# Layer 0's output weights split at the start and loaded back in pieces, with the first modulation blocks at high priority

## The chip, the cores and the metric

The kernel runs on one core of one Trainium2 chip. The metric is the device time of one execution in microseconds (us); the median of several runs counts. The engines are TensorE (PE, with its weight loads apart as PEld), VectorE (DVE), ScalarE (ACT), GpSimd (POOL) and SyncE (SP), whose queue issues almost all DMAs.

## What is computed

The reference is a backbone of two layers over 2048 latent tokens and 256 context tokens with 1024 channels (2304 rows in all). Layer 0 feeds a latent attention of 8 heads (MLA) and a bidirectional mLSTM of 4 heads from one projection, layer 1 a gated linear attention and a neighbourhood attention. Each layer modulates its normalised input by a vector from `c`, multiplies the joined heads by a gate and projects them with `w_out`:

```python
cq, ckv, k_rope, mq, mk, mv, mo, gates, z = split_cols(u @ w_in, EVEN_SPLITS)
...
a_lat = block_attention(qa_l, jnp.concatenate([ka_c, ka_l], axis=2), jnp.concatenate([va_c, va_l], axis=2), scale)
...
h_c, h_l = bidirectional_scan(mlstm_chunked, init, seq_c, gates_c, seq_l, gates_l)
...
hm = head_rmsnorm(jax.nn.sigmoid(mo.astype(jnp.float32)) * merge_heads(h), h_norm, MLSTM_HEADS).astype(dtype)
return (jnp.concatenate([merge_heads(a), hm], axis=-1) * jax.nn.silu(z)) @ w_out
```

## The kernel before

Rows are tiled by 128. A float32 matrix product is made of fp16 parts: weights and inputs are scaled by a power of two and split into a high part and the remainder (`wh`, `wl`, `uh`, `ul`), and three products are added in PSUM. For the big input projection (`gemm_in`, "the gemm" below) `weights_` does this for each block of columns: load `wr` (L288), maximum of magnitudes on DVE (L290), scale (`pow2_scale`, L145 to L153: a small chain of PE and DVE), scaling and high part on ACT (L299, L300), remainder on POOL (L301). The products are L322 (columns in the rows, 128x384) and L343 (tokens in the rows, 128x256); their results leave PSUM by ACT (L278) or DVE (L276), and go to DRAM scratch (`scr_mqk`, `scr_rpg` from L328, `scr_z` from L361).

Layer 0's input stage (`layer0_in`) has the following parts. At the opening `prep_u0` computes the modulation (`mods`: `c` is loaded, its tanh taken at L103, 2 MB blocks `wm` of the modulation weights are loaded at L115, multiplied at L122 and gathered at L126 and L133), and its columns (`prep_cols`), and normalises the input (L187, L191, L80 to L87). Then layer 1's output weights are split by `out_weights`: eight loads `owr` of 512 KB (L1001), eight maxima on DVE (L1003), the scale, and for each of the eight the high part on ACT (L1016) and the remainder on DVE (L1017), stored to scratch `w1hl` (L1019). Then come the mLSTM's convolution, gates (L832 to L897, with loads `gbi`, `gA`, `gB` and transposes L887 on PE) and scan (from L951), and the preparation of the latent attention (`mla_prep`: projections L489, keys and queries stored at L498, values by L515, stored at L389).

Then layer 0's own output weights are split by the same function (`out_setup0`), with the results kept in SBUF (`owh`, `owl`) until the projection behind the attention. The attention (`mla_attn`) needs, for each block of 512 queries of a head, the maximum of each query's scores first (`qmax`: matmul L578, DVE maximum L579) and then scores (L613 to L615), exponentials (L618) and values (L633). Keys `kk` are loaded at L561, values `v` at L564, queries `qq` at L569; 34 units of maxima are computed before the main loop. The first `kk` lies in memory that the `owr` buffers of `out_setup0` use before it; the second `kk` lies where layer 0's input `uh`, `ul` was, which the gemm reads to its end. After the lead come the last gemm blocks (`mo` and `z`), and the mLSTM's norm (`mlstm_norm`: loads `hf` L1047, `hb` L1048, `mo` L1049, sum on POOL L1050, product on DVE L1051, norm L1059, store L1060), then the attention's main loop, with PE in an order written by hand. `finish` writes 40 blocks `att0` (5 of each head).

The order of instructions on each queue is set at build time by a scheduler that simulates the engines: it takes code in the order traced, lets later code go ahead where an engine would wait, and lets code under `high_priority` go first. So the gemm is filler: its blocks stand between the parts of the other stages. SBUF pools are placed on two sides; a new tile waits for the last reader of the memory that it takes.

## Time and profile before

| | |
|---|---|
| Median of 3 runs | 3649.45 us (3647.62 to 3654.1) |
| Profiled execution | 3645.0 us, its span 3642.7 us |
| Mean granted clock of PE | 0.974 |
| Busy: PE, DVE, ACT, POOL | 3391.9, 2563.9, 1832.6, 972.9 us |
| Mean DMA rate | 137 GB/s |

In the rows below, "busy" is the time in which an engine works, "idle before <-X" the time that it stood still ahead of an instruction and what ended that. The granted clock is a share of 2.4 GHz. Shares of DMA are those of 16 DMA engines.

### The profile page before, as it was taken

The page shows a single profiled execution, that of the slowest core. Times are in us where ns is not written, and L with a number is a line of the kernel's source. Part 1 is how long each engine was busy: PE and PEld are TensorE (multiplying, and loading weights), DVE is VectorE, ACT ScalarE, POOL GpSimd, SP SyncE. Part 2 cuts the span into 40 slices and gives each one's busy share as a digit, 9 for nine tenths or more (in the row PEclk, how much of TensorE's full clock was granted, in tenths as well). Part 3 has the DMA queues.
Part 4 walks back from the last instruction along what each step waited for, and adds up shares of the span by engine and source line. Part 5 has one row for each costly group of instructions (what it writes and reads, how often), then busy time and mean ns, then how long its engine had stood idle before and what let it go on. Part 6 is the DMA issues. An engine that isn't in the chain of part 4 may idle for free.

```text
span 3642.7 us, 77364 instructions
## 1 busy us (share of the span) xinstructions
PE 3391.9 (93%) x30588; PEld 2575.3 (71%) x30588; DVE 2563.9 (70%) x5697; ACT 1832.6 (50%) x3243; POOL 972.9 (27%) x908
## 2 busy tenths in 40 slices
PE   6999999999888899999999999999888899899898
PEld 3566888898556677777777555676565789898754
DVE  5657576678766888888887566354688547776887
ACT  4333323334443577777777433256465435455632
POOL 1012204473221233333333222101355322111122
PEclk8999999999999799999999999999999999999999
DMA  7632347776778222221110543227554545437343
GB/s 264 242 122 69 141 179 227 222 234 218 215 225 231 77 49 52 53 49 47 31 47 14 168 152 121 66 83 211 166 160 133 144 98 145 123 96 194 117 164 122
DMA packets 400535, 498.35 MB, mean 137 GB/s; under 512 B 104110, under 2 KB 306339, under 8 KB 394988
## 3 DMA queue, kind: packets, MB, share of 16 engines
q1 hardware_dynamic: 400172, 493.40, 44.7%
q8 instruction: 241, 3.95, 0.5%
q14 instruction: 122, 1.00, 0.1%
HBM read 311.73 MB, written 181.43 MB: 135 GB/s over the span
## 4 chain that ended last, share of the span: by engine, by line
PE 58%; DVE 20%; DMA 12%; issue 5%; ACT 4%; POOL 1%; SPq 1%; POOLq 0%; DVEq 0%; ACTq 0%
PE ps L343 13%; PE ps L322 8%; PE po L633 5%; PE ops L1119 4%; PE pm L578 4%; PE ps L613 3%; PE ps L615 3%; PE ps L614 3%; PE t L1544 2%; DVE mc L579 1%; PE s L1522 1%; PE o L1560 1%; PE s L1523 1%; DMA scr_mqkc<-y 1%; PE ps L489 1%
## 5 line engine op out<-in xcount | busy, mean ns | idle before, releaser
L343 PE MATMUL ps<-wh,uh 128*128 128x256 f16 (+3 forms) x2816 | 742.6, 269 | 33.8 <-ACT ot L278 13.0
L343 PE MATMUL ps<-wl,uh 128*128 128x256 f16 (+3 forms) x2816 | 741.6, 268 | 0.0
L343 PE MATMUL ps<-wh,ul 128*128 128x256 f16 (+3 forms) x2816 | 736.3, 268 | 1.4 <-POOL ul L210 1.4
L343 PEld LDWEIGHTS <-uh 128*128 128x128 f16 x5632 | 532.1, 99 | 118.2 <-issue 43.4
L579 DVE TENSOR_REDUCE mc<-pm 128x1 f32<-128x512 f32 (+1 forms) x656 | 403.2, 628 | 115.5 <-PE pm L578 107.3
L618 ACT ACTIVATE p<-ps 128x1024 f32<-128x1024 f32 (+1 forms) x296 | 299.8, 1013 | 158.8 <-PE ps L615 119.2
L322 PE MATMUL ps<-uh,wh 128*128 128x384 f16 (+2 forms) x1008 | 323.9, 325 | 7.5 <-DVE ofs L332 2.8
L322 PE MATMUL ps<-ul,wh 128*128 128x384 f16 (+2 forms) x1008 | 326.1, 326 | 1.1 <-DVE ul L210 1.1
L322 PE MATMUL ps<-uh,wl 128*128 128x384 f16 (+2 forms) x1008 | 325.7, 325 | 0.0
L622 POOL TENSOR_TENSOR pl<-p,ph 128x1024 f16<-128x1024 f32 (+1 forms) x98 | 207.9, 2122 | 434.8 <-ACT ph L619 416.5
L619 ACT CAST ph<-p 128x1024 f16<-128x1024 f32 (+1 forms) x296 | 306.4, 1035 | 7.6
L343 PEld LDWEIGHTS <-ul 128*128 128x128 f16 x2816 | 277.6, 99 | 37.7 <-POOL ul L210 2.6
L322 PEld LDWEIGHTS <-wh 128*128 128x128 f16 (+1 forms) x2016 | 198.2, 100 | 134.8 <-issue 24.0
L578 PE MATMUL pm<-kk,qq 96*128 96x512 f32 (+1 forms) x656 | 271.5, 418 | 21.4 <-DVE mc L579 15.8
L622 DVE TENSOR_TENSOR pl<-p,ph 128x1024 f16<-128x1024 f32 (+1 forms) x198 | 244.4, 1236 | 27.7 <-ACT ph L619 23.0
L301 POOL TENSOR_TENSOR wl<-wr,wh 128x2048 f16<-128x2048 f32 (+4 forms) x31 | 121.3, 3914 | 492.8 <-ACT wh L300 431.0
L633 PE MATMUL po<-v,ph 128*128 128x129 f16 x2336 | 246.8, 221 | 0.0
L613 PE MATMUL ps<-qq,kk 96*128 96x512 f32 (+1 forms) x592 | 240.5, 406 | 0.0
L633 PEld LDWEIGHTS <-pl 128*128 128x128 f16 x2336 | 196.6, 98 | 61.2 <-issue 58.9
L633 PE MATMUL po<-v,pl 128*128 128x65 f16 x2336 | 237.4, 194 | 0.4 <-DVE pl L622 0.4
L615 PE MATMUL ps<-qq,kk 98*128 98x512 f32 (+1 forms) x592 | 233.1, 394 | 0.0
L614 PE MATMUL ps<-qq,kk 96*128 96x512 f32 (+1 forms) x592 | 232.4, 393 | 0.0
(429 smaller groups left out, 7997.3 us busy)
## 6 DMA issues: line engine op xcount, KB each, us to landing
wr<-in_l_w_in_dram SPq DMA_DIRECT2D x26, 1024.0 KB
wm<-in_l_w_mod_dram SPq DMA_DIRECT2D x12, 2048.0 KB
z<-scr_z SPq DMA_DIRECT2D x34, 512.0 KB
scr_z<-ot SPq DMA_DIRECT2D x44, 384.0 KB
k<-scr_nk SPq DMA_DIRECT2D x14, 1152.0 KB
scr_mqk<-of SPq DMA_DIRECT2D x48, 192.0 KB
x<-scr_mqk SPq DMA_DIRECT2D x8, 1152.0 KB
scr_mqkc<-y SPq DMA_DIRECT2D x8, 1152.0 KB
```

What stands on the lines that cost most here:

```text
L322: nc.tensor.matmul(ps[0:m, t0:BLK], w_[:, k, m0:m0 + m], u_[:, k, t0:BLK], start=(q == 0), stop=(q == 3 * KT - 1))
L343: nc.tensor.matmul(ps[:, 0:n], u_[:, k, i * P:(i + 1) * P], w_[:, k, 0:n], start=(q == 0), stop=(q == 3 * KT - 1))
L578: nc.tensor.matmul(pm[:, 0:n], qq[0:96, 0, s * P:(s + 1) * P], kk[0:96, 0, u * 512:u * 512 + n], start=True, stop=True)
L579: nc.vector.reduce_max(mc[:, s, u:u + 1], pm[:, 0:n], AX.X)
L613: nc.tensor.matmul(pj[:, 0:nq], kk[0:96, 0, ks], qq[0:96, 1, 0:nq], start=True, stop=False)
L614: nc.tensor.matmul(pj[:, 0:nq], kk[0:96, 1, ks], qq[0:96, 0, 0:nq], start=False, stop=False)
L615: nc.tensor.matmul(pj[:, 0:nq], kk[0:98, 0, ks], qq[0:98, 0, 0:nq], start=False, stop=True)
L618: nc.scalar.activation(p32[:, :, 0:nq], ps[:, :, 0:nq], AF.Exp, scale=scale)
L619: nc.scalar.copy(ph[:, :, 0:nq], p32[:, :, 0:nq])
L622: eng.tensor_tensor(pl[:, :, 0:nq], p32[:, :, 0:nq], ph[:, :, 0:nq], ALU.subtract)
L633: nc.tensor.matmul(o_, p_[:, j, s * P:(s + 1) * P], v[:, kt, 0:w], start=w == 129 and kt == 0 and s % 2 == 0, stop=w == 129 and kt == kts[ ...
L1119: nc.tensor.matmul(ps, c_[:, k], w_[k][:, ns], start=(q == 0), stop=(q == 3 * KT - 1))
```

## The change

Three things are changed. First, layer 0's output weights are split right after layer 1's, by the same function and into a new DRAM scratch `w0hl`; the scale is kept in a small tile `ows0`. `out_setup0` only takes the SBUF tile `owhl` for them, which has the size of `owh` and `owl`, and it is filled in the attention: 16 loads of 256 KB, one behind each store of `att0` from the sixth on, ordered behind it on SP's queue. Second, in `prep_u0` the two calls of `mods` and `prep_cols` are traced at high priority. Third, the remainder of the input weights on POOL is made in eight pieces for the weights that are traced before `prep_u0` has put its input there (`u[1]` is None), which are the first two; the others keep one instruction.

```diff
             sink = mk(name="pu_mp", bufs=1, space=PSUM).tile([P, 256, 2], F32, name="pmod")[:, 0:16]
-            mods((2, 3), sink)
+            with tc.high_priority():
+                mods((2, 3), sink)
             nxt = load_block(0)
-            mods((0, 1), sink)
-            last = self.dma_mods
-            m4, out[1] = self.prep_cols(0, cp, up, pp, sink)
+            with tc.high_priority():
+                mods((0, 1), sink)
+                last = self.dma_mods
+                m4, out[1] = self.prep_cols(0, cp, up, pp, sink)
...
-            nc.gpsimd.tensor_tensor(wl[:, :, 0:n], wr[:, :, 0:n], wh[:, :, 0:n], ALU.subtract)
+            step = 1 if u[1] is None else KT
+            for k in range(0, KT, step):
+                nc.gpsimd.tensor_tensor(wl[:, k:k + step, 0:n], wr[:, k:k + step, 0:n], wh[:, k:k + step, 0:n], ALU.subtract)
...
+                fin[0] += 1
+                k = fin[0] - 6
+                if 0 <= k < 2 * KT:
+                    with tc.issue_after(st.ins):
+                        nc.sync.dma_start(self.hl0[:, k // KT, k % KT], S["w0hl"][:, k // KT, k % KT])
...
-                self.nc.vector.tensor_copy(self.ows1, self.out_weights(1, xp, xp, ops, S["w1hl"]))
+                for i, ows in ((1, self.ows1), (0, self.ows0)):
+                    self.nc.vector.tensor_copy(ows, self.out_weights(i, xp, xp, ops, S[f"w{i}hl"]))
...
-            w0 = self.out_setup0()
+            *w0, hl = self.out_setup0()
...
-        with tc.tile_pool(name="opx0", bufs=2, side="right") as xp, tc.tile_pool(name="opp0", bufs=2, space=PSUM, side="right") as ops:
-            w = self.out_weights(0, cpw, xp, ops)
-        return e0, cpw, w
+        hl = cpw.tile([P, 2, KT, D], F16, name="owhl")
+        return e0, cpw, ([hl[:, 0, k] for k in range(KT)], [hl[:, 1, k] for k in range(KT)], self.ows0), hl
```

Lines behind the edits move down; L1001 is L1013 in the changed kernel, L1019 is L1024, L561 is L566, L578 is L583, L343 is L348, L613 is L618.

What stands on each engine's queue is shown at three places. The first is ACT's opening, before (`th` is the tanh of `c`, `wr` and `wh` the first weight, `sqj` the normalisation):

```order
L103 ACT_TABLE_LOAD
L103 ACTIVATE th<-c_177 16x128
L299 ACTIVATE wr<-wr,wsc 128x2048
L300 CAST wh<-wr 128x2048
L187 ACTIVATE sqj,ssq<-x 128x1024 x5
```

The same of the changed kernel:

```order
L302 ACT_TABLE_LOAD
L302 ACTIVATE wr<-wr,wsc 128x2048
L104 ACTIVATE th<-c_193 16x128
L303 CAST wh<-wr 128x2048
L188 ACTIVATE sqj,ssq<-x 128x1024 x4
```

The tanh has moved behind the scaling of the first weight; on SP the first `wm` stands ahead of `c`.

The second place is SP's queue at the early split, before (rows 61 on; `scr_mqk` are the gemm's stores, `wr` the gemm's next weight):

```order
L1001 DMA owr<-in_l_w_out_dram 128x1024 x8
L328 DMA scr_mqk<-of 128x384 x6
L1019 DMA scr_w1hl<-ohl 256x1x1024
L328 DMA scr_mqk<-of 128x384
L1019 DMA scr_w1hl<-ohl 256x1x1024
L288 DMA wr<-in_l_w_in_dram 128x8x256
```

Of the changed kernel, from the same load on:

```order
L1013 DMA owr<-in_l_w_out_dram 128x1024 x8
L333 DMA scr_mqk<-of 128x384 x6
L1024 DMA scr_w1hl<-ohl 256x1x1024
L1013 DMA owr<-in_l_w_out_dram 128x1024
L1024 DMA scr_w1hl<-ohl 256x1x1024
L1013 DMA owr<-in_l_w_out_dram 128x1024
L291 DMA wr<-in_l_w_in_dram 128x8x256
```

A load of layer 0's weights now follows each store of layer 1's; eight stores `w0hl` come after these, ahead of the gates' loads. On PE the first transpose of the gates (L887) stands behind 1239 gemm matmuls, where it stood behind 1027.

The third place is SP's queue on the way into the attention, before (`scr_v` are the stores of the values, `gate` and `hm` those of the output stage and the mLSTM):

```order
L1001 DMA owr<-in_l_w_out_dram 128x1024 x6
L389 DMA scr_v_70<-ov_10347 128x8x129
L1001 DMA owr<-in_l_w_out_dram 128x1024 x2
L1048 DMA hb<-scr_h_76 128x512
L139 DMA gate<-scr_mods_57 128x1024
...
L1048 DMA hb<-scr_h_76 128x512
L561 DMA kk_10435<-scr_kn 64x4608
L562 DMA kk_10435<-scr_kr 32x4608
L564 DMA v<-scr_v_70 128x2322 x2
```

Of the changed kernel:

```order
L394 DMA scr_v_70<-ov_10420 128x8x129
L566 DMA kk_10459<-scr_kn 64x4608
L567 DMA kk_10459<-scr_kr 32x4608
L140 DMA gate<-scr_mods_57 128x1024
L1064 DMA scr_hm<-hf 128x512
L394 DMA scr_v_70<-ov_10432 128x8x129
```

The loads of `kk` have moved up to the last store of the values; the eight loads of `owr` are gone from there. On PE, 282 gemm matmuls follow the last L515, where 417 did, and eight of the query maxima stand among them, where two did. In the attention the list differs by the 16 loads alone, and after it in nothing.

## Rows read from the trace of the kernel before

**Rows 1.** page: engines' busy time; shares of the chain that ended last

```profile
PE 3391.9 (93%) x30588; PEld 2575.3 (71%) x30588; DVE 2563.9 (70%) x5697; ACT 1832.6 (50%) x3243; POOL 972.9 (27%) x908
...
PE 58%; DVE 20%; DMA 12%; issue 5%; ACT 4%; POOL 1%; SPq 1%; POOLq 0%; DVEq 0%; ACTq 0%
```

**Rows 2.** windows: PE, PEld, DVE, ACT, POOL busy; clock, DMA share, GB/s

```profile
1128.90:1187.80 58.90, 48.95 (x424) 42.22 (x422) 40.38 (x87) 20.56 (x48) 4.67 (x4) 0.97 0.89 245
1187.80:1219.60 31.80, 21.31 (x38) 9.23 (x37) 25.25 (x61) 3.58 (x15) 3.27 (x2) 0.55 0.49 134
```

**Rows 3.** chain of waits, 1120 to 1225: start us, us, what it is

```profile
1171.25 1.19 DVE owl L1017
...
1173.77 10.49 DMA v<-scr_v
...
1188.98 10.41 DMA hf<-scr_h
...
1220.24 0.43 PE pm L578
```

**Rows 4.** timeline of PE: start, us, engine, line, operation, tiles, count, [idle before]

```profile
1128.78 0.27 PE L343 MATMUL ps<-wh,uh 128*128 128x256 f16 x1
...
1129.98 0.27 PE L343 MATMUL ps<-wh,ul 128*128 128x256 f16 x1
...
1184.32 0.77 PE L578 MATMUL pm<-kk,qq 96*128 96x256 f32 x2 [4.68 <-DMA v<-scr_v]
...
1187.47 0.29 PE L343 MATMUL ps<-wh,ul 128*128 128x256 f16 x1
...
1202.27 0.58 PE L578 MATMUL pm<-kk,qq 96*128 96x256 f32 x1 [3.71 <-DVE mc L579]
1204.58 1.22 PE L578 MATMUL pm<-kk,qq 96*128 96x512 f32 x2 [1.72 <-DVE mc L579]
...
1219.39 0.41 PE L613 MATMUL ps<-qq,kk 96*128 96x256 f32 x1
```

**Rows 5.** timeline of SP's queue, around the loads for the attention

```profile
1131.08 3.92 SPq L1001 DMA_DIRECT2D owr<-in_l_w_out_dram  x6
...
1172.47 0.48 SPq L561 DMA_DIRECT2D kk<-scr_kn  x1
```

**Rows 6.** windows of the mLSTM scan and of the attention's preparation

```profile
560.00:900.00 340.00, 329.21 (x2961) 302.83 (x2959) 235.58 (x779) 137.91 (x403) 171.89 (x231) 0.99 0.72 228
900.00:1130.00 230.00, 199.44 (x1350) 133.47 (x1349) 164.19 (x469) 101.65 (x290) 47.48 (x53) 0.98 0.75 222
```

**Rows 7.** groups of instructions, 160 to 260 us: busy, mean ns | idle before

```profile
L1017 DVE SCALAR_TENSOR_TENSOR ohl<-owr,ows,ohl 128x1024 f16<-128x1024 f32 x8 | 10.2, 1283 | 7.6 <-ACT ohl L1016 7.6
...
L1016 ACT ACTIVATE ohl<-owr,ows 128x1024 f16<-128x1024 f32 x8 | 9.1, 1146 | 13.4 <-DMA scr_w1hl<-ohl 8.2 <-DVE ows L153 5.1
L1003 DVE TENSOR_REDUCE omx<-owr 128x1 f32<-128x1024 f32 x7 | 8.2, 1212 | 0.0
```

**Rows 8.** windows of the gemm around the early split, of the attention

```profile
160.00:240.00 80.00, 80.00 (x493) 50.72 (x491) 36.24 (x70) 32.49 (x32) 13.51 (x5) 1.00 0.50 170
...
1440.00:1980.00 540.00, 529.05 (x4809) 420.81 (x4807) 456.33 (x711) 421.42 (x451) 181.40 (x119) 1.00 0.17 41
```

**Rows 9.** timeline of the opening, by engine: PE, ACT, DVE, POOL

```profile
12.14 3.64 PE L122 MATMUL mps<-wm,sT 128*32 128x512 f32 x16 [1.20 <-DMA wm<-in_l_w_mod_dram]
...
50.55 0.58 PE L151 MATMUL ps<-pw_sc,ones 1*128 1x2 f32 x2 [4.45 <-DVE pw_sc L150]
...
6.34 1.28 ACT L103 ACT_TABLE_LOAD   x1 [6.34 <-DMA c<-in_c_ctx_dram]
...
11.18 2.00 ACT L299 ACTIVATE wr<-wr,wsc 128x2048 f32<-128x2048 f32 x1 [3.23 <-DVE wsc L153]
...
46.35 3.69 DVE L85 TENSOR_TENSOR rs_t<-rstd 128x3 f32<-128x3 f32 x1
...
45.94 4.08 POOL L301 TENSOR_TENSOR wl<-wr,wh 128x2048 f16<-128x2048 f32 x1 [26.69 <-ACT wh L300]
```

More of the change, by code (lines that the diff above doesn't have):

```diff
@@ L73, in __init__ @@
         self.glss = self.const.tile([P, 16, 4], F32, name="glss")
+        self.ows0 = self.const.tile([P, 2], F32, name="ows0")
         self.ows1 = self.const.tile([P, 2], F32, name="ows1")
@@ L600, in qmax_row @@
                     nc.sync.dma_start(qq[96 + a:97 + a, 0, 0:nq].bitcast(F32).rearrange("o (s p) -> o s p", p=P), mt[0:ns, a].bitcast(F32))
-            cnt = [0]
+            cnt, fin = [0], [0]
             def qk(blk, pr, mid):
@@ L650, in finish @@
                 nc.gpsimd.tensor_tensor(ob[:, 0:na], ob[:, 0:na], rc[:, 0:na].broadcast_to([P, na, 2, 64]), ALU.mult)
-                nc.sync.dma_start(S["att0"][q0:q0 + nq, h * 64:(h + 1) * 64].rearrange("(s p) d -> p s d", p=P),
-                                  ob[:, 0:na].rearrange("p a b d -> p (a b) d"))
+                st = nc.sync.dma_start(S["att0"][q0:q0 + nq, h * 64:(h + 1) * 64].rearrange("(s p) d -> p s d", p=P),
+                                       ob[:, 0:na].rearrange("p a b d -> p (a b) d"))
+                fin[0] += 1
[3 more added lines that the diff above has]
+                        nc.sync.dma_start(self.hl0[:, k // KT, k % KT], S["w0hl"][:, k // KT, k % KT])
             todo = []
@@ L783, in layer0_in @@
             self.mlstm_norm()
+        self.hl0 = hl
         return w0, attn
@@ L992, in mlstm_scan, with out_weights @@
                 step(back[i], 1)
-    def out_weights(self, layer, cp, xp, pp, dst=None):
+    def out_weights(self, layer, cp, xp, pp, dst):
         nc, I = self.nc, self.I
@@ L1005, in out_weights @@
         ws = self.pow2_scale(cp, pp, mx[:, KT:KT + 1], "ows", "ops")
-        if dst is None:
-            wh = cp.tile([P, KT, D], F16, name="owh")
-            wl = cp.tile([P, KT, D], F16, name="owl")
         for k in range(KT):
             wr = wrs[k]
-            if dst is None:
-                h, l = wh[:, k], wl[:, k]
-            else:
-                hl = xp.tile([P, 2, D], F16, name="ohl")
-                h, l = hl[:, 0], hl[:, 1]
+            hl = xp.tile([P, 2, D], F16, name="ohl")
+            h, l = hl[:, 0], hl[:, 1]
             nc.scalar.activation(h, wr, AF.Copy, scale=ws[:, 0:1])
             nc.vector.scalar_tensor_tensor(l, wr, ws[:, 0:1], h, ALU.mult, ALU.subtract)
-            if dst is not None:
-                nc.sync.dma_start(dst[:, :, k], hl)
-        return ([wh[:, k] for k in range(KT)], [wl[:, k] for k in range(KT)], ws) if dst is None else ws
+            nc.sync.dma_start(dst[:, :, k], hl)
+        return ws
     def out_setup0(self):
@@ L1710 @@
     "gq": (256, T), "gk": (256, T), "gva": (T, 544), "gla": (SEQ, 512), "glB": (P, 4, T), "glZ": (NT, P, 4, P),
-    "w1hl": ((P, 2, KT, D), F16), "nq": (512, 2, T), "nk": (512, 2, T), "nv16": ((8, P, NT, 129), F16), "z1": (T, 1024), "na": (SEQ, 512),
+    "w0hl": ((P, 2, KT, D), F16), "w1hl": ((P, 2, KT, D), F16), "nq": (512, 2, T), "nk": (512, 2, T), "nv16": ((8, P, NT, 129), F16), "z1": (T, 1024), "na": (SEQ, 512),
 }
```

## The prediction

> **What bounds the kernel now.** I read the page first: busy times and the chain that ended last. TensorE (PE) is busy 93% of the span and holds 58% of the chain, VectorE (DVE) 20% [rows 1]. So an edit can win only where PE stands still, or runs slowly because it stood still; DVE, ACT or DMA time beside a busy PE is worth nothing. Next I looked for the stretches where PE stands still. The one that the change aims at is the passage into layer 0's attention, from the last value projection (L515, its last matmul gives way to gemm at 1128.8 us, T0 below) to the first score matmul L613 at 1219.4 [rows 4]. In its first part PE is busy 48.95 of 58.9 us, in its second 21.31 of 31.8 at a granted clock of 0.55 [rows 2]. What holds it up is told by the chain of waits and SP's queue: `owr` loads go out at 1131.08 and SP hands out the first `kk` load at 1172.47 only, right after the last L1017 has let go of the memory in which `kk` is to lie (1171.25 and 1.19 in the chain) [rows 3, 5]. Then `v` takes 10.49 us and PE waits 4.68 us for it [rows 3, 4]. In the second part, PE waits on the DVE maxima (L579), with one gap around 1202 where DVE itself stood behind an `hf` load of 10.41 us [rows 3, 4].
>
> The sum is made on the profiled execution: 3645.0 us, 2.3 of them outside its span of 3642.7. The median of the runs is 3649.45, so 4.45 us go on top at the end.
>
> **The passage into the attention.** First what it costs now, clean. Between T0 and the first L613 the order has 417 gemm matmuls (L343) and 35 query-maximum matmuls (L578), two of the latter ahead of the last 13 gemm matmuls. A gemm matmul takes 0.109 us (eleven steps between 1128.78 and 1129.98) [rows 4]; a maximum behind the gemm takes 0.82 (18 of them between 1204.58 and 1219.39, paced by DVE) [rows 4]. 417 x 0.109 = 45.5, 33 x 0.82 = 27.1, together 72.6; it took 90.6, so 18.0 us are waits and low clock: 4.7 for `v`, 4.7 in the tail (31.8 - 27.1) [rows 2], 8.6 in the gemm, beside the reductions, the splitting and the `owr` loads.
>
> After the change the `owr` loads, L1003, L1016 and L1017 are gone from there and `kk` stands on SP ahead of the last `v16` store. Only 282 gemm matmuls are left after the last L515 (30.7 us), eight maxima lie among them (six more than now, 0.43 us each at full clock [rows 3], 2.6), and 27 follow at 0.82 (22.1). That is 55.4 plus waits, s, against 90.6. The 135 gemm matmuls that are no longer there were not dropped; the order has them before T0, which moves T0 by 14.7. The gain is 90.6 - 55.4 - 14.7 - s = 20.5 - s.
>
> What is late next sets s. `hf` is: in the new order one L1051 comes among the gemm's last evictions, and another behind the 25th maximum; its `hf` load stands on SP behind `kk` of the second head (which waits for the last gemm matmul, since its memory is that of layer 0's input), a `wr` load and two stores, of which one waits for L1059 on DVE. This is the same wait as now, 4.7. In the gemm 2 of the 8.6 stay, for `scr_z` stores. I take s = 7, with bounds of 3 (`hf` in time) and 18 (as much as now).
>
> A second term, i: the earlier gemm work has to fit where PE has room. By the order, weighted with columns, the gemm work done before the scan rises by 24 us, but that inside scan and preparation (first L951 to last L515) falls by 9.8, of which 5.4 lie in the preparation. The scan leaves PE idle 10.8 of 340 us: less filler makes it shorter. The preparation leaves it idle 30.6 of 230 [rows 6]: there others set the pace, and less filler makes more idle time. So i lies between 0 and 9.8; I take 3, about half of the preparation's share. Gain: 20.5 - 7 - 3 = **10.5 us**, bounds 17.5 and -7.3.
>
> **The early split.** Eight L1003 (1.212), eight L1017 (1.283) and eight L1016 (1.146) move to about 200 to 240 us: 20.0 us of DVE, 9.2 of ACT [rows 7], with 4 MB read and 4 MB written. PE is busy there 80.00 of 80 us, DVE 36.24, ACT 32.49, DMA 0.50 [rows 8], so there is room for all of it. Not free is the gates' chain, which on DVE and SP now stands behind it (`gbi` and `gA` loads behind the eight `w0hl` stores). Its first PE part, L887, now stands behind 1239 gemm matmuls instead of 1027, some 34 us later, which covers 20 us of DVE and about as much of waiting. Below nothing it cannot go, as PE has no idle time to give back there. I take **+2**, bounds 0 and 20.
>
> **The opening.** First, the modulation. `wm` now precedes `c` on SP, and on ACT the tanh of `c` (L103; its table load was done at 6.34) stands behind L299, which runs from 11.18 to 13.18; the first mods matmul waits today for `wm` alone, at 12.14 [rows 9]. Tanh, its multiplication, a transpose and a copy then put it at about 14.6: +2.5. That is felt only if the loads whose buffers it frees, and what waits for them, slip too: between 0 and 2.5; I take 1. Second, the pieces of L301. A one-vector L85 on DVE takes 3.69 us at 46.35 and ends at 50.04, while POOL's L301 runs from 45.94 to 50.02; PE's L151 waits 4.45 us for what stands behind that L85 [rows 9]. With eight pieces of about 0.51 (4.08 / 8) DVE can come in between, and up to 3.5 us are won; I take 2.5. The opening then gives **-1.5**, bounds -3.5 and +4.
>
> This second step is one on which the Trainium skill speaks against the change ("SBUF — State Buffer", section "Who interferes with whom"): a DVE instruction with two SBUF inputs and a GpSimd instruction that reads SBUF exclude each other, and whichever began first holds the ports to its end. The trace agrees (50.04 against 50.02). By that rule each of the ten or so short two-input instructions that DVE has there could be stopped once for up to one piece, and the opening would come to +1.5 or more instead of -1.5.
>
> **Pieces in the attention.** 16 loads of 256 KB, one behind each `att0` store from the sixth to the twenty-first, about 0.4 us of SP each. DMA is used to 0.17 there [rows 8], and nothing reads them before the projection behind the attention: 0. After the attention the order is the same.
>
> **Sum.** -10.5 + 2 - 1.5 = -10.0: 3635.0 in the profile, 3639.5 against the median. The forecast's own range, from s of 4 to 11 and i of 0 to 6, is 3633 to 3646.
>
> **Rivals.**
> *The full gain.* `hf` arrives in time (s = 3), scan and preparation shrink with their filler (i = 0), the split is hidden, and the opening gives 3.5: -17.5 - 3.5 = -21, 3628.5. For it: the `owr` loads leave a DMA share of 0.89 in the first part [rows 2]. Against it: the `hf` load behind `kk`, `wr` and two stores.
> *The gain given back.* Today's waits come back in other names (s = 16: two L1051 waits, `kk`, `v` and eight query loads at once) and the preparation idles (i = 6): 20.5 - 22 = -1.5, so +1.5 - 1.5 + 2 = +2, or 0 with the split at nothing: 3649.5 to 3651.5. For it: DVE, not the loads, paced the tail at 0.82 [rows 4].
> *Slower: the early split holds up the gates.* If the 20 us of DVE work, with `w0hl` stores ahead of `gbi` and `gA` on SP, delay L887 by more than the 34 us of gemm matmuls that cover it, PE stands still in front of it. It decides the sign when the stall passes 12 us; with all 20 on the path and the opening at +0, -10.5 + 20 + 1.5 = +11: 3660.5. For it: DVE already idled there for stores and loads [rows 7]. Against it: PE is never idle there and the order has put gemm work ahead.
> *The opening backfires.* High priority moves the blocks' tables behind a weight; tanh late, pieces alternating: +4 in place of -1.5, net -4.5, 3645. Then the part that is named for it doesn't do what it says.
>
> **How the numbers follow.** Forecast 0.45, full gain 0.17, given back 0.21, opening 0.04, slower 0.13. No change means within 0.2% (7.3 us), about what a measurement of this kernel can tell: 3642.2 to 3656.7. Of the forecast 0.35 lies below that band and 0.10 in it. Faster: 0.35 + 0.17 = 0.52; same: 0.10 + 0.21 + 0.04 = 0.35; slower 0.13. The range, 3625 to 3657, takes in the whole of the forecast and of the gain given back and most of the full gain, and leaves out the slower case and the extremes, about 0.18.
>
> **What would show it.** Right: in the changed kernel's trace `kk` is issued within 5 us of T0, the first L613 comes 62 us after T0, and T0 lies 15 to 20 us later than 1128.8; PE is full between 160 and 240; L85 at some 46 us is short. Wrong: PE idle before L887; a gap over 8 us in front of the second L1051 in the tail; more than 35 us idle in the preparation; a first mods matmul that delays the first L322.

## The result and the profile after

The changed kernel takes **3675.06 us** (median; 3663.75 to 3678.34) where the kernel before takes 3649.45 (3642.46 to 3661.56): a ratio of 1.0065, 95% interval 1.0053 to 1.0076. It is slower, by some 25 us, where a gain of 10 was forecast. The profiled executions show the same sign: a span of 3675.9 us against 3642.7. They lie 33 us apart, some 8 more than the medians, so the starts below carry that much of single executions.

The page of the changed kernel, busy times and shares of the chain that ended last:

```profile
PE 3395.7 (92%) x30588; PEld 2578.8 (70%) x30588; DVE 2555.5 (70%) x5698; ACT 1832.9 (50%) x3243; POOL 975.4 (27%) x922
...
PE 48%; DVE 18%; DMA 13%; issue 5%; ACT 3%; POOL 2%; SPq 1%; POOLq 0%; DVEq 0%; ACTq 0%
```

Beside [rows 1] no engine has much more work: DVE has 8 us less, PE 4 more. So the time is in waits. The table cuts both executions at the same instructions (starts in us, lines of before):

| | before | after | later by |
|---|---|---|---|
| first gemm matmul L322 | 54.6 | 54.5 | -0.1 |
| first maximum of the early split, L1003 | 157.9 | 160.4 | 2.5 |
| first transpose of the gates, L887 | 275.7 | 324.0 | 48.3 |
| scan begins, L951 | 564.3 | 598.8 | 34.5 |
| scan ends | 835.5 | 877.8 | 42.3 |
| T0, last L515 | 1128.6 | 1168.9 | 40.3 |
| attention's first L613 | 1219.4 | 1248.5 | 29.1 |
| layer 0's projection, first L1119 | 2020.6 | 2049.4 | 28.8 |
| end | 3642.0 | 3675.2 | 33.2 |

Windows between these points, before (us; then PE, PEld, DVE, ACT and POOL busy; clock, DMA share, GB/s): early split to gates, scan, scan to T0, passage, attention.

```profile
157.90:275.70 117.80, 113.75 (x694) 70.95 (x692) 70.47 (x108) 43.59 (x46) 13.51 (x5) 0.99 0.40 138
...
564.30:835.50 271.20, 265.50 (x2383) 246.77 (x2383) 185.03 (x623) 105.42 (x317) 151.55 (x209) 1.00 0.75 233
835.50:1128.60 293.10, 258.03 (x1854) 184.94 (x1852) 213.19 (x618) 133.40 (x374) 65.97 (x74) 0.97 0.72 219
1128.60:1219.40 90.80, 70.36 (x462) 51.43 (x461) 65.62 (x148) 24.14 (x62) 8.24 (x6) 0.82 0.75 206
1219.40:2020.60 801.20, 785.43 (x7158) 624.74 (x7157) 660.34 (x1028) 629.21 (x674) 268.81 (x177) 0.99 0.17 42
```

The same of the changed kernel:

```profile
160.40:324.00 163.60, 147.66 (x884) 90.18 (x882) 97.80 (x132) 57.79 (x63) 18.31 (x6) 0.98 0.49 166
...
598.80:877.80 279.00, 265.75 (x2328) 245.19 (x2328) 191.05 (x631) 105.53 (x321) 153.33 (x209) 0.99 0.74 228
877.80:1168.90 291.10, 253.06 (x1795) 179.77 (x1793) 203.97 (x589) 126.23 (x363) 60.77 (x71) 0.97 0.73 210
1168.90:1248.50 79.60, 53.15 (x324) 37.47 (x323) 42.85 (x131) 14.43 (x50) 7.95 (x6) 0.74 0.75 175
1248.50:2049.40 800.90, 785.04 (x7157) 623.73 (x7155) 661.61 (x1035) 629.55 (x674) 268.50 (x177) 1.00 0.20 49
```

The loss is in the first row. The gates begin 48.3 us later: 34 us of PE's work more stand ahead of them (147.66 against 113.75), and PE stands still 15.9 us of this stretch instead of 4.0. The filler that went ahead is missing behind, so gates to scan is 13.8 us shorter, but the scan has as much PE work as before and takes 7.8 longer (idle 13.25 against 5.70). At T0 40 us are lost. The passage gives back 11.2, not the 28 of the forecast, and attention and what follows give back nothing.

What stands on DVE and ACT ahead of the gates now, groups of 160 to 260 us (busy, mean ns | idle before, what ended it), to be read beside [rows 7]:

```profile
L1023 DVE SCALAR_TENSOR_TENSOR ohl<-owr,ows,ohl 128x1024 f16<-128x1024 f32 x16 | 23.2, 1464 | 15.5 <-ACT ohl L1022 15.5
L1022 ACT ACTIVATE ohl<-owr,ows 128x1024 f16<-128x1024 f32 x16 | 18.0, 1143 | 24.7 <-DMA scr_w0hl<-ohl 10.2 <-DVE ows L154 6.3 <-DMA scr_w1hl<-ohl 5.3
```

Sixteen pairs instead of eight, each pair through one of two `ohl` buffers: ACT waits 15.5 us for their stores, DVE 15.5 for ACT. The last L1023 starts at 256.26 where the last L1017 of before was at 199.83, and the gates' work stands behind it.

In the passage (timelines of SP, DVE and PE; start, us, engine, line):

```profile
1172.93 1.21 SPq L566 DMA_DIRECT2D kk<-scr_kn  x1
...
1175.11 0.43 SPq L140 DMA_DIRECT2D gate<-scr_mods  x1
...
1190.67 0.75 DVE L1037 TENSOR_SCALAR gate<-gate,ows 128x1024 f32<-128x1024 f32 x1 [10.87 <-DMA gate<-scr_mods]
...
1192.21 0.37 PE L348 MATMUL ps<-wh,uh 128*128 128x256 f16 x1 [5.01 <-DVE ot L279]
...
1193.62 0.33 SPq L569 DMA_DIRECT2D v<-scr_v  x1
...
1200.30 0.77 PE L583 MATMUL pm<-kk,qq 96*128 96x256 f32 x2 [5.80 <-DMA qq<-scr_qr]
...
1231.54 1.80 DVE L293 TENSOR_REDUCE wmx<-wr 128x1 f32<-128x352 f32 x4 [7.13 <-DMA wr<-in_l_w_in_dram]
...
1240.94 0.69 DVE L1055 SCALAR_TENSOR_TENSOR hf<-mo,hf 128x512 f32<-128x512 f32 x1 [0.62 <-POOL hf L1054]
```

`kk` is early, 4 us behind T0 instead of 44 [rows 5]. In its place three other loads are late. The `gate` load, issued behind `kk`, holds DVE 10.87 us in L1037, and PE 5.01 us behind it; the store of `scr_v` takes 17.43 us beside `kk`, `v` waits for it on SP and `qq` stands behind `v`, so PE waits 5.80; then DVE waits 7.13 for the weight `wr`, which was issued behind the second `kk`. In the place of the `hf` wait that I had named, DVE waits 0.62.

The opening (timelines of PE, POOL and DVE):

```profile
14.11 3.64 PE L123 MATMUL mps<-wm,sT 128*32 128x512 f32 x16 [0.35 <-DVE sT L110]
...
43.90 5.06 POOL L306 TENSOR_TENSOR wl<-wr,wh 128x256 f16<-128x256 f32 x8 [23.86 <-ACT wh L303]
...
47.76 0.59 DVE L87 SCALAR_TENSOR_TENSOR rs_t<-rs_t,rs_ms 128x3 f32<-128x3 f32 x1
...
48.39 0.59 DVE L88 SCALAR_TENSOR_TENSOR rstd<-rs_t,rstd 128x3 f32<-128x3 f32 x1
...
48.48 0.37 PE L146 MATMUL ps<-ident,mx 128*1 128x128 f32 x1 [4.34 <-DVE mx L178]
```

The one long L85 of 3.69 us [rows 9] is gone, but five one-vector operations of DVE (L82, L83, L86, L87, L88) now take 0.59 to 0.62 us each, as long as a POOL piece (5.06 / 8 = 0.63; 0.51 was forecast). PE waits 4.34 us for `mx` and 1.11 for the scale behind it, where it waited 1.09 and 4.45: 5.45 instead of 5.54. The first mods matmul is at 14.11, before at 12.14. The first gemm matmul comes out 0.1 us earlier: nothing, as the executions below put it anywhere between 53.1 and 55.5, and at 53.1 in `e2_move`, which lacks the new opening.

### The profile page after: what moved, and what is told of

Its sections match the earlier page's. It is cut to its first block, busy times and chain, and to the rows that moved or that the text cites. A ratio compares the mean times of both kernels' runs of the same rounds, so it can differ in the third digit from the quotient of the medians.

```text
span 3675.9 us, 77440 instructions
## 1 busy us (share of the span) xinstructions
PE 3395.7 (92%) x30588; PEld 2578.8 (70%) x30588; DVE 2555.5 (70%) x5698; ACT 1832.9 (50%) x3243; POOL 975.4 (27%) x922
## 4 chain that ended last, share of the span: by engine, by line
PE 48%; DVE 18%; DMA 13%; issue 5%; ACT 3%; POOL 2%; SPq 1%; POOLq 0%; DVEq 0%; ACTq 0%
PE ps L348 11%; PE po L638 5%; PE ops L1123 4%; PE ps L327 4%; PE pm L583 3%; PE ps L618 3%; PE ps L620 3%; PE ps L619 3%; DMA wr<-in_l_w_in_dram 2%; PE t L1548 2%; DVE mc L584 1%; DMA scr_v<-ov 1%; PE s L1526 1%; PE o L1564 1%; PE s L1527 1%
## 5 line engine op out<-in xcount | busy, mean ns | idle before, releaser
L348 PE MATMUL ps<-wh,uh 128*128 128x256 f16 (+3 forms) x2816 | 742.6, 269 | 34.6 <-DVE ot L279 12.8
L348 PE MATMUL ps<-wl,uh 128*128 128x256 f16 (+3 forms) x2816 | 741.1, 268 | 0.0
L348 PE MATMUL ps<-wh,ul 128*128 128x256 f16 (+3 forms) x2816 | 736.5, 268 | 1.9 <-POOL ul L211 1.9
L348 PEld LDWEIGHTS <-uh 128*128 128x128 f16 x5632 | 531.6, 99 | 119.9 <-issue 45.8
L348 PEld LDWEIGHTS <-ul 128*128 128x128 f16 x2816 | 277.4, 99 | 38.4 <-POOL ul L211 2.9
L583 PE MATMUL pm<-kk,qq 96*128 96x512 f32 (+1 forms) x656 | 270.1, 415 | 29.0 <-DVE mc L584 21.3
L306 POOL TENSOR_TENSOR wl<-wr,wh 128x2048 f16<-128x2048 f32 (+5 forms) x45 | 123.0, 2747 | 521.4 <-ACT wh L303 515.4
L618 PE MATMUL ps<-qq,kk 96*128 96x512 f32 (+1 forms) x592 | 240.4, 406 | 0.0
```

Source lines behind the costliest of these rows:

```text
L348: nc.tensor.matmul(ps[:, 0:n], u_[:, k, i * P:(i + 1) * P], w_[:, k, 0:n], start=(q == 0), stop=(q == 3 * KT - 1))
L583: nc.tensor.matmul(pm[:, 0:n], qq[0:96, 0, s * P:(s + 1) * P], kk[0:96, 0, u * 512:u * 512 + n], start=True, stop=True)
L618: nc.tensor.matmul(pj[:, 0:nq], kk[0:96, 0, ks], qq[0:96, 1, 0:nq], start=True, stop=False)
```

## The experiments

Two theories. **A, the chain:** gates, convolution, scan, preparation and passage hang on each other; PE looks full there because the gemm fills it, and what delays the gates delays the attention. **B, PE's work:** PE is the bound, and the loss is waits at the passage and PE idle time. Each ratio is against the kernel before on the same chip, with its 95% interval; the plain quotient of two medians differs from it by up to 0.11%. Diffs are against the changed kernel unless said, and show the main lines only; `...` marks what is left out.

### One part alone

`e1_opening` is the kernel before with the high priority and the POOL pieces; `e2_move` the changed kernel without these two.

```diff
-                mods((2, 3), sink)          # e1: under tc.high_priority(), as in the changed kernel
...
-            nc.gpsimd.tensor_tensor(wl[:, :, 0:n], wr[:, :, 0:n], wh[:, :, 0:n], ALU.subtract)
+            step = 1 if u[1] is None else KT
...
```

> The kernel before with the second and third part of the change alone (modulation blocks at high priority, POOL remainder in pieces); the output weights stay where they were. Theory (the loss of about 25 us comes from moving the weights): no difference, -3 to +3 us against before, first L322 at 54 to 55 us as in both kernels. Rival (the opening's new order costs later stages): 8 to 25 us slower than before.

> The changed kernel without the second and third part: only the output weights are moved and loaded back in pieces. Theory (the move alone carries the loss): 20 to 30 us slower than before, like the whole change. Rival (the opening carries it): within 5 us of before.

Measured: e1 0.9999 (0.9988 to 1.0011), e2 1.0053 (1.0038 to 1.0068). The opening has no effect that shows within some 4 us; the moved split carries the loss.

### No split of layer 0's weights

```diff
-                for i, ows in ((1, self.ows1), (0, self.ows0)):
+                for i, ows in ((1, self.ows1),):
...
-                        nc.sync.dma_start(self.hl0[:, k // KT, k % KT], S["w0hl"][:, k // KT, k % KT])
+                        nc.sync.dma_start(self.hl0[:, k // KT, k % KT], S["w1hl"][:, k // KT, k % KT])
...
```

> The changed kernel with layer 0's split left out altogether; the attention loads layer 1's split weights in its place, so 8 MB of transfers, 20 us of DVE and 9 us of ACT are gone from 180 to 260 us. Theory (the early split stalls PE ahead of the gates, by 12 us, and the rest of the loss is in the scan and at the passage): 10 to 15 us faster than the whole change, PE idle before the first L899 down from 16 to about 5 us, the passage into the attention still about 80 us long. Second theory (the scan's 8 us of extra idle follow from the split as well): 18 to 25 us faster. Rival (the split is hidden, the loss is a matter of the order that the scheduler chose): under 5 us faster.

Measured: 0.9980 (0.9970 to 0.9989). That is 0.85% or 31 us below the changed kernel. Windows, early split to gates and passage:

```profile
160.20:277.60 117.40, 110.56 (x672) 68.90 (x671) 69.05 (x103) 42.06 (x44) 14.09 (x5) 0.98 0.40 136
...
1128.40:1206.20 77.80, 63.02 (x458) 48.75 (x457) 44.49 (x126) 16.15 (x54) 7.47 (x6) 0.88 0.73 179
```

The gates start at 277.6, T0 is at 1128.4 as before, and the emptied passage takes 77.8 us instead of 90.8. So the gain that the change is after exists, 13 us in the passage and about 7 in the total, and the early split costs some 31, four times as much. PE's order up to T0 is that of before here: the profiles have 1438 matmuls ahead of the first L887, before 1436, the changed kernel 1650. So it is the split that brings the gemm work ahead of the gates in the changed kernel.

### The waits at the passage

`e4_gate` puts the `gate` load behind the thirtieth `att0` store; `w16_gq` does so too and issues the first `v` behind `qq` (on top of `w16_6`, below).

```diff
...
-                        gate = self.out_gate(0, 1 if t == 0 else 0, cpw, w[2])
+                        with tc.issue_after(self.att_st.ins) if t == 0 else ExitStack():
+                            gate = self.out_gate(0, 1 if t == 0 else 0, cpw, w[2])
```

> The changed kernel with the load of layer 0's output gate, and with it L1037 on DVE, held back until the 30th store of the attention. Theory (DVE stood 10.9 us behind that load, the gemm's PSUM results behind DVE, and PE 5 us and more behind these): 5 to 9 us faster than the whole change, no PE wait over 1 us between 1180 and 1192 us. Rival (the next wait, for the queries' loads behind the store of the last values, takes the gain): under 3 us faster, the wait before the first L583 grows from 5.8 to over 10 us.

> The run with 16 and 6 buffers, and with two loads out of the way at the passage: the output gate behind the 30th store of the attention, the first queries ahead of the first values. Theory (DVE waits for the gate, PE for the queries behind the store of the last values): 4 to 9 us faster than the run with 16 and 6 buffers alone, the passage from last L515 to first L613 68 to 74 us instead of 78. Rival (one wait passes into the next): within 3 us of it.

Measured: e4 1.0086 (1.0071 to 1.0101). Its passage is shorter, 73.9 us:

```profile
1166.60:1240.50 73.90, 52.27 (x324) 37.10 (x323) 44.50 (x134) 14.31 (x50) 7.95 (x6) 0.77 0.75 183
```

PE's idle time falls from 26.5 to 21.6, by the 5 us that it waited behind L1037, and the total gains nothing. `w16_gq`, 1.0069 (1.0054 to 1.0083), has a passage of 79.3 against 79.8 of `w16_6`. PE's 4.5 us behind L279 are gone there, but its wait for `qq`, 2.7 us in `w16_6`, has grown although `qq` now goes out ahead of `v`:

```profile
PE pm L581 <- DMA qq<-scr_qr: 9.7, 1, 9.7
```

Theory B's first half falls: 25 us are not lost here.

### Are the buffers to blame?

`w16_6` loads all sixteen `owr` into buffers of their own, takes both maxima and scales first and gives `ohl` six buffers; `w16_nost` leaves out the stores of `w0hl` too (the attention then loads layer 1's).

```diff
-            wr = xp.tile([P, D], F32, name="owr", bufs=KT)
+            wr = xp.tile([P, D], F32, name="owr", bufs=16)
...
-            hl = xp.tile([P, 2, D], F16, name="ohl")
+            hl = xp.tile([P, 2, D], F16, name="ohl", bufs=6)
...
-            nc.sync.dma_start(dst[:, :, k], hl)        # w16_nost only
+            if layer:
+                nc.sync.dma_start(dst[:, :, k], hl)
```

> The changed kernel with the same work in the early split, but 16 instead of 8 buffers for the loads and 6 instead of 2 for the split results, and both layers' maxima and scales traced ahead of both splits. Theory (the early split costs by its waits for buffers, a round trip through eight load buffers and two result buffers, which held the queues of DVE, ACT and SP until 257 us): first L887 back at 275 to 285 us, 25 to 32 us faster than the whole change, so 0 to 9 us faster than before. Rival (20 us of DVE work, 9 us of ACT work and 8 MB of transfers are the price, whatever the buffers): under 10 us faster than the whole change, first L887 at 305 us or later.

> The run with 16 and 6 buffers without the eight stores of layer 0's split (the attention loads layer 1's split weights in their place); loads, maxima, ACT and DVE work are all there. Theory (SP's queue: the gemm's next weight stands behind stores that wait for the split's results, so weights come late and PE stands still): PE idle between first owr maximum and first L887 from 26 to under 12 us, first L887 at 278 to 288, total 3636 to 3648. Rival (DVE and ACT themselves, whose queues hold the gemm's own maxima and scaling behind the split): idle still over 20 us, first L887 at 296 us or later, total over 3652.

Measured: 1.0067 (1.0051 to 1.0083) and 1.0067 (1.0053 to 1.0082). The order of the gemm is that of before again, and PE now stands still instead: window of `w16_6`, early split to gates, and its longest waits there (us, times, longest).

```profile
163.70:302.40 138.70, 112.19 (x651) 68.73 (x650) 88.61 (x126) 49.14 (x51) 14.04 (x5) 0.89 0.49 174
```
```profile
PE ps L146 <- DVE wmx L294: 11.9, 1, 11.9
PE ps L146 <- DVE of L279: 6.0, 1, 6.0
```

26.5 us of it are idle: the gemm's next weight, `wmx`, waits behind the split. In `w16_nost` (PE's longest wait; SP, DVE and ACT):

```profile
PE pt L809 <- DMA rowsel<-in_rowsel_dram: 8.7, 1, 8.7
```
```profile
161.42 13.11 SPq L1016 DMA_DIRECT2D owr<-in_l_w_out_dram  x16
...
184.58 0.14 DVE L154 COPY ows<-ops 128x2 f32<-128x2 f32 x1
...
184.80 6.34 ACT L1026 ACTIVATE ohl<-owr,ows 128x1024 f16<-128x1024 f32 x6 [20.34 <-DMA scr_mqk<-of]
```

Without the stores it idles as long (gates at 304.8): SP needs 13.11 us to hand out the sixteen loads, and ACT stands still for 20.34 us. The profile puts that down to a store of the gemm behind the loads, but the scale of the split (L154) is ready only 0.08 us ahead of L1026, and the same wait in `w16_gq`, 20.45 us, is put down to L154: ACT's queue waits for the maxima of the weights. More buffers bring another delay of the same size.

### Which part of the split

`s_max` adds to `e3_nosplit` loads, maxima and scale of layer 0's weights; `s_act` also ACT's high parts; `a_nost` also DVE's remainders, so that only the stores are missing; the changed kernel has all. None of the three stores `w0hl`.

```diff
+        for k in range(KT if layer else 0):                     # s_max
...
             if layer:                                           # s_act
+                nc.vector.scalar_tensor_tensor(l, wr, ws[:, 0:1], h, ALU.mult, ALU.subtract)
...
+            if layer:                                           # a_nost
+                nc.sync.dma_start(dst[:, :, k], hl)
```

> The changed kernel with only the loads, maxima and the scale of layer 0's weights at the start: the eight L1022, eight L1023 and the eight stores are left out (the attention loads layer 1's split weights in their place). Theory (what holds the gates up is the second half, whose results wait for two buffers and their stores): within 8 us of the run without any of layer 0's split, so 3634 to 3644 us, first L887 at 278 to 286. Rival (the loads that wait for layer 1's buffers are what holds up SP's and DVE's queues): half of the loss or more, 3650 to 3668, first L887 at 300 us or later.

> The run a_nost with the eight remainders on DVE (L1023) left out as well: of the second half of layer 0's split ACT's eight L1022 alone are there. If DVE's 10 us are the price: first L899 from 313 to 300 us or earlier and 10 us or more faster than a_nost, so 3650 to 3656. If ACT's part, or the order that the scheduler chose for a split at this place (186 us of gemm ahead of the first L899 instead of 167), is the price: first L899 at 308 to 316 us, within 6 us of a_nost.

> The changed kernel without the eight stores of layer 0's split (the attention loads layer 1's split weights in their place); 8 load and 2 result buffers, maxima, ACT and DVE work as in the whole change. Theory (two result buffers, each held until its 512 KB store has landed, stretch the second half, and that is most of the loss): first L899 from 324 to 305 us or earlier, 15 us or more faster than the whole change. Rival (DVE, ACT and the loads are enough): first L899 after 316 us, within 6 us of the whole change.

Windows, early split to gates, of the three in this order:

```profile
159.80:289.50 129.70, 116.34 (x692) 71.12 (x690) 81.23 (x119) 41.56 (x45) 14.05 (x5) 0.97 0.45 157
```
```profile
160.70:311.50 150.80, 137.58 (x811) 83.68 (x809) 81.94 (x119) 56.41 (x60) 18.98 (x6) 0.95 0.44 148
```
```profile
160.50:313.30 152.80, 137.42 (x811) 83.49 (x809) 94.72 (x127) 56.22 (x60) 18.96 (x6) 0.97 0.43 146
```

| | gates begin | first L613 | ratio to before |
|---|---|---|---|
| e3_nosplit | 277.6 | 1206.2 | 0.9980 (0.9970 to 0.9989) |
| s_max | 289.5 | 1217.5 | 0.9991 (0.9981 to 1.0002) |
| w16_6 | 302.4 | 1240.2 | 1.0067 (1.0051 to 1.0083) |
| w16_nost | 304.8 | 1243.4 | 1.0067 (1.0053 to 1.0082) |
| s_act | 311.5 | 1232.1 | 1.0040 (1.0026 to 1.0054) |
| a_nost | 313.3 | 1237.2 | 1.0050 (1.0034 to 1.0065) |
| e2_move | 316.8 | 1230.3 | 1.0053 (1.0038 to 1.0068) |
| changed | 324.0 | 1248.5 | 1.0065 (1.0053 to 1.0076) |

Loads and maxima add 0.11%, ACT's eight activations 0.49%, DVE's remainders 0.10%, the stores 0.15%, each as a difference of two ratios. Only ACT's step, at 9 us of work, is clear of the intervals; how the rest divides is not shown. At ACT's step the order of the gemm changes (811 matmuls ahead of the gates for 692). Over the whole table, gates that begin 12 to 46 us later than in `e3_nosplit` bring an attention that begins 11 to 42 us later (0.6 to 1.4 us for each), whether gemm work stands ahead of them (`s_act`) or PE idles (`w16_6`). This is what theory A says. The total follows less closely (1.0067 with the gates at 302.4, 1.0053 with 316.8).

### The split in other places

`p_gates` writes layer 0's split behind the gates; `a_split2` puts it wholly into the attention, through two buffers, one piece behind each `att0` store.

```diff
...
                 gates = self.mlstm_gates(kp)
+                with tc.tile_pool(name="opx2", bufs=2, side="right") as xp0, tc.tile_pool(name="opp2", bufs=1, space=PSUM, side="right") as ops0:
+                    self.nc.vector.tensor_copy(self.ows0, self.out_weights(0, xp0, xp0, ops0, S["w0hl"]))
...
-                        nc.sync.dma_start(self.hl0[:, k // KT, k % KT], S["w0hl"][:, k // KT, k % KT])   # a_split2
+                own(fin[0] - 3, st)     # load, L1003; after the eighth the scale; load again, L1016, L1017
```

> The changed kernel with layer 0's split written behind the mLSTM's gates instead of ahead of them. Theory (the split stands in front of whatever the program names next, and that chain is what the later stages wait for): first L887 at 278 us as before, but first L951 some 40 us later than before, and the total as slow as the whole change, 3660 to 3680. Rival (only the gates are sensitive): first L951 under 15 us later, 3635 to 3650.

> Layer 0's whole split is done inside the attention: behind the 3rd to 10th store of att0 a piece of the weights is loaded and its maximum taken, behind the 11th the scale is made, behind the 12th to 19th the piece is loaded again and split by ACT and DVE straight into its place in SBUF; no scratch, nothing of it at the start or at the passage. Theory (the same 20 us of DVE and 9 us of ACT cost nothing where PE alone is the bound and the others have room, as the attention with DVE busy 82% and ACT 79%): attention 800 to 806 us long, first L1119 at 2005 to 2014 us, 2 to 12 us faster than before. Rival (the attention's order has no room, each piece stops the exponentials and so PE): the attention grows by 15 to 30 us, 3 to 20 us slower than before.

Measured: `p_gates` 1.0099 (1.0083 to 1.0115). The gates begin at 277.3, but the scan at 614.2, 50 us later than before, and T0 at 1177.0. The delay sits wherever the split is in front of the chain. Its passage has hardly any gemm left, and is still long:

```profile
1177.00:1248.90 71.90, 31.09 (x109) 16.93 (x108) 35.54 (x104) 6.91 (x27) 6.69 (x5) 0.57 0.77 169
```

`a_split2`, 1.0052 (1.0037 to 1.0066): the attention begins at 1203.2, earlier than anywhere above, and takes 30 us longer. Window of the attention and two waits in it:

```profile
1203.20:2034.80 831.60, 797.87 (x7161) 630.85 (x7160) 682.07 (x1052) 636.25 (x682) 269.02 (x177) 0.98 0.21 52
```
```profile
PE pm L583 <- DVE mc L584: 17.3, 21, 2.7
...
PE pm L146 <- DVE omx L647: 7.6, 1, 7.6
```

DVE's 20 us stand ahead of the query maxima that PE waits for (7.8 us in 11 waits before), and the chain of the scale stops PE once for 7.6. In a stretch where PE is busy 785 of 801 us, DVE's time beside it was not free.

### Is PE's work the bound at all?

`t_cut` is `e3_nosplit` with one product instead of three in the last `z` block, 288 matmuls fewer at the passage (129 left instead of 417); `t_cut3` does so for the two `mo` blocks too: another 576 fewer, 576 x 0.109 = 63 us of PE, and no gemm matmul is left at the passage.

```diff
-                        for w_, u_ in ((wh, uh), (wl, uh), (wh, ul)):
+                    tri = ((wh, uh), (wl, uh), (wh, ul))[0:1 if c0 == 3504 else 3]      # t_cut3: c0 in (2208, 2464, 3504)
+                        for w_, u_ in tri:
```

> The run without any of layer 0's split (e3_nosplit) with 288 gemm matmuls less at the passage: the last block of z0's columns is made with one of its three products, so 129 instead of 417 gemm matmuls follow the last L520; everything up to there is as in that run. The prediction's working (the passage is gemm matmuls at 0.109 us plus maxima at 0.82 plus waits) gives 31 us less: 77.8 to about 46 us from last L520 to first L619. Theory now (the passage has a floor, set by the stores and loads of keys, values and queries and by the chain of maxima, and the gemm only fills it): 66 to 74 us, PE idle there 30 to 40 instead of 15.

> The run t_cut with the two column blocks of mo at one product instead of three as well: 576 gemm matmuls less than in t_cut, of which the order takes 42 us out of the attention's preparation (first L495 to last L521) and the rest out of the passage, where none are left. If PE's work set the time there, preparation and passage would shrink by 42 and 14 us against t_cut. Theory (a chain of dependent steps sets it and the gemm only fills): the preparation goes from 212 to 195 to 208 us, the passage stays at 64 to 72, total 0 to 25 us faster than t_cut.

Measured: 0.9932 (0.9910 to 0.9954) and 0.9933 (0.9919 to 0.9947). The first 31 us of PE work taken away give 17 us, the next 63 give nothing (the intervals leave some 10 us either way). Passage and attention of `t_cut`, then scan, passage and attention of `t_cut3`:

```profile
1120.50:1190.70 70.20, 40.91 (x171) 24.16 (x169) 41.55 (x117) 15.99 (x54) 7.87 (x6) 0.67 0.81 193
1190.70:1990.80 800.10, 784.02 (x7158) 622.83 (x7157) 660.69 (x1040) 629.28 (x674) 269.05 (x177) 1.00 0.20 49
```
```profile
558.90:844.00 285.10, 272.19 (x2386) 249.73 (x2384) 203.65 (x676) 120.36 (x355) 156.20 (x210) 0.99 0.76 236
1118.50:1175.20 56.70, 23.76 (x41) 10.34 (x40) 31.60 (x95) 5.08 (x27) 5.94 (x5) 0.52 0.69 164
1175.20:1987.50 812.30, 789.46 (x7157) 625.18 (x7155) 673.82 (x1080) 632.24 (x698) 274.25 (x180) 0.99 0.21 52
```

By the prediction's 0.109 each, `t_cut`'s passage should fall by 31 us; it fell by 7.6, and 29 of its 70 us are idle. The less gemm there is, the more PE stands still and the lower the granted clock: 0.88 with 63.0 us busy of 77.8 (`e3_nosplit`), 0.67 with 40.9 of 70.2, 0.52 with 23.8 of 56.7; 1.0 is the 2.4 GHz level, 0.5 the 1.2 GHz one. In `t_cut3` the preparation, from the first L489 to T0, is 18 us shorter than in `t_cut`, but the scan takes 285.1 instead of 271.0: with as many matmuls in it (x2386, x2387 in `t_cut`) it holds more blocks and so more of their evictions, 203.65 us of DVE instead of 185.68. The passage, which I had expected at 64 to 72, is 13.5 us shorter than in `t_cut`, but the attention is 12.2 longer: part of the mLSTM's norm has moved into it (twelve L1059 instead of four). The Trainium skill ("Perfetto Trace Analysis", section "Identifying the Most-Contended Engine") would have one work first on the engine that is occupied most, TensorE's headroom being judged by its share of peak operations or its weight loads. By busy time that is PE here (93%), by weight loads (71%) PE and DVE (70%) [rows 1] are level. These runs show where such a rule ends: 576 matmuls less of the busiest engine gave nothing.

### The trade that pays

`sw_gemm0`: layer 0's weights alone are split early, and layer 1's, which are needed much later, behind the first gemm columns of layer 1; `sw_gemm3` puts them behind its fourth.

```diff
-                for i, ows in ((1, self.ows1), (0, self.ows0)):
+                for i, ows in ((0, self.ows0),):
...
                 gemm(0)
+                with tc.tile_pool(name="opx2", bufs=2, side="right") as xp1, tc.tile_pool(name="opp2", bufs=1, space=PSUM, side="right") as ops1:
+                    nc.vector.tensor_copy(self.ows1, self.out_weights(1, xp1, xp1, ops1, S["w1hl"]))
```

> The two splits trade places: layer 0's alone stands at the start, where layer 1's stood, and layer 1's is written behind layer 1's first gemm columns, where DVE is busy 10 of 50 us and PE all the time. Theory (one split at the start is covered, a second one is not; the gain at the passage is that of the run without layer 0's split): first L613 at 1200 to 1212 us, and 0 to 10 us faster than before if the split is covered at its new place too. Rival (a split costs 20 us or more wherever PE has no second stream of work): 10 to 25 us slower than before, the loss between first L1119 and first L1522.

> As the run sw_gemm0, with layer 1's split written later, behind layer 1's last gemm columns ahead of the neighbourhood attention. Theory: first L613 at 1200 to 1212 us; there DVE is busy 12 of 50 us at 2900 us, so 0 to 10 us faster than before. Rival: 10 to 25 us slower than before, the loss between first L1522 and the end.

Measured: `sw_gemm0` **0.9970 (0.9959 to 0.9981)**, 3633.11 us: faster than both kernels. Early split to gates, passage, and layer 1 up to the first L1522:

```profile
160.30:278.50 118.20, 110.92 (x674) 68.94 (x673) 68.30 (x103) 42.02 (x44) 14.10 (x5) 0.98 0.40 136
1122.90:1200.50 77.60, 62.97 (x459) 48.67 (x458) 44.67 (x127) 16.14 (x54) 7.80 (x6) 0.88 0.74 180
2002.70:2913.40 910.70, 838.99 (x8875) 576.28 (x8875) 579.75 (x1349) 415.18 (x916) 255.60 (x220) 0.98 0.49 151
```

The gates are in time and the passage is as short as in `e3_nosplit`. Layer 1's stretch takes 910.7 us instead of 897.3 before, but what follows L1522 takes 707.2 instead of 724.1: the filler put ahead there is saved later, and with two splits the kernel is no slower than `e3_nosplit` with one (0.9980). `sw_gemm3` is slower, 1.0072 (1.0060 to 1.0085), through that stretch (window, longest wait, and SP's queue):

```profile
2006.10:2986.50 980.40, 867.96 (x9082) 603.16 (x9082) 594.20 (x1371) 422.70 (x927) 269.37 (x234) 0.95 0.46 141
```
```profile
PE s L1528 <- DMA v<-scr_nv: 40.0, 1, 40.0
```
```profile
2947.52 24.63 SPq L1024 DMA_DIRECT2D scr_w1hl<-ohl  x8
...
2978.20 0.59 SPq L1505 DMA_DIRECT2D v<-scr_nv  x1
```

PE waits 40 us at once for a `v` that stands behind the split's eight stores on SP. What follows L1522 is 41 us shorter, half of the loss of 83. The same work costs nothing in one place and 37 us (1.02% between the two) in the other.

## Why the prediction was wrong

**The step that failed is the early split: +2 stood there, with ends of 0 and 20, and it costs some 31.** I read PE full and DVE, ACT and DMA half used [rows 8], and went by the sentence that DVE, ACT or DMA time beside a busy PE is worth nothing. But PE was busy with gemm that any other moment would have taken, while the gates' chain stood behind the split on DVE and SP. The 34 us of matmuls that I let cover the split were no cover: they are most of the delay, and where the order keeps them back, PE idles instead for the same loss (`w16_6`). What the gates lose is still lost at the first L613 for the most part (table above).

**The price of moved matmuls failed with it.** 0.109 us each was to be returned at the passage, 14.7 in all. They were paid at T0 and hardly returned: the changed kernel's passage, with 282 gemm matmuls, takes 79.6 us, that of `e3_nosplit`, with all 417, 77.8; that of `e2_move`, with some 60 fewer than the changed kernel's, 69.1. `t_cut` agrees, where 288 matmuls taken away there gave 7.6 us and became idle time at a lower clock for the rest; `p_gates`, with 109 matmuls of any kind left there, still took 71.9. No run shows one fixed floor. T0 was put 17.7 us later and came 40.3 later: 16.0 of PE work, near the 14.7 of the forecast, 11.9 more of PE idle in front of the gates, 7.5 more idle in the scan, 3.0 more between scan and T0, 1.9 elsewhere. The idle time in scan and preparation is the term i: it was 3, with an end of 9.8, and is 10.5, where I had let less filler shorten the scan.

**s was 7 and became 24:** the passage takes 79.6 us, 55.4 of them counted matmuls. I had named `hf`; the waits are for `gate` behind the first `kk`, `qq` behind the store of `scr_v`, and `wr` behind the second `kk`. The rival "given back" (16) was nearer, but this did not decide: `e4_gate` shortened the passage by 6 us for nothing in the total.

**The opening was -1.5 and shows no effect** (`e1_opening`, 0.9999, some 4 us either way). The Trainium skill's rule on the shared port ("SBUF — State Buffer", "Who interferes with whom") agrees with the trace: DVE's short operations there with two inputs (L86 to L88) take as long as one of POOL's pieces, 0.59 to 0.62 beside 0.63 us. So do L82 and L83, with one input, for which the rule as I used it says nothing. Cutting the instruction spread the wait instead of removing it; -1.5, 0 and +1.5, the sum by the rule, are closer together than `e1_opening` can tell apart.

**The slower rival was right in its place, wrong in its form and its size.** I let it begin with PE idle over 12 us in front of L887, and priced it at 20; 11.9 us more are idle there, and the larger part is gemm work put ahead. (Its total of +11 also counted +1.5 for an opening said to be at +0; it is +9.5.) I spoke against it that the order "has put gemm work ahead", which is the very delay.

**Right were** `kk` 4 us behind T0, the short L85, the attention untouched by its 16 loads (800.9 us against 801.2), nothing new after it beyond the spread of single executions (1625.8 us against 1621.4, 1624.9 in `e3_nosplit`), and, with no early split, a gain of 13.0 us in the emptied passage, for which 20.5 - 7 = 13.5 stood in the sum.

**Still open** is why ACT's eight activations alone cost 0.49%, more than their 9 us. In `s_act` the order itself changes (1.0040), in `w16_6` it does not, and the whole split loses as much (1.0067) as in the changed kernel (1.0065); no run separates the order from ACT's queue.

## What to carry to other kernels

Where a large product fills the gaps between dependent stages, a full PE doesn't tell that other engines' work beside it is free: look for the stage that the next one waits for, and count what a moved step puts in front of it on every queue. Compare the start of each stage before and after; a delay that stays the same through several stages belongs to a chain, and the place where it arises is the place to change. Move work to where nothing soon depends on its queues: of two equal splits, the one needed later should go later, and where, within one layer, decided between a gain of 0.3% and a loss of 0.7% here.

## What the runs showed of the hardware

- Sixteen loads of 512 KB at once took SP 13.11 us to issue (`w16_nost`), and all that stands behind them on the queue goes out later by that.
- The last store of the values took 17.43 us beside the first `kk` loads (chain of waits of the changed kernel).
- In runs with the same order on PE up to T0, T0 lay between 1120.5 and 1128.4 us (`t_cut`, `sw_gemm0`, `e3_nosplit`): a single profile places an instruction at 1100 us only to some 8 us, so that differences of a few us between stages were read only together with the medians.
